# Swapping the two hardware DMA queues of a softmax kernel: loads on ScalarE, stores on Sync

## The chip, the cores and the metric

The kernel runs on one core of a Trainium2 chip. The metric is the device time of one execution in microseconds (us).

A ratio below is the mean time of one kernel's fast runs over the mean of the other kernel's fast runs in the same rounds on the same chip. It is therefore not quite the ratio of the medians quoted beside it. The range in brackets is its 95% interval.

## The reference

```python
# x: (16, 1024, 512) float32
x_scaled = x / 0.5
x_max = np.max(x_scaled, axis=-1, keepdims=True)
exp_x = np.exp(x_scaled - x_max)
return exp_x / np.sum(exp_x, axis=-1, keepdims=True)
```

This is a softmax over the last axis: 33.55 MB are read and as much is written.

## The kernel before

The 16384 rows are cut into eight chunks of 128 partitions x 16 rows x 512 elements (4096 KB each). Six buffers hold them, and everything is computed in place. Chunks 6 and 7 take the buffers of chunks 0 and 1, so their loads must wait until those have been stored. The last row of chunk 7 comes by a separate path on GpSimd.

```python
LOADS = [[(0, 4), (4, G)]] + [WHOLE] * 6 + [[(0, G - 1)]]
BLOCKS = [[(0, 4), (4, 8), (8, G)]] + [WHOLE] * 6 + [[(0, 8), (8, G)]]
STORES = [WHOLE] * 8
BUFS = 6
# ... (cut)
warm = stats.tile([P, 1], fp32, name="warm", bufs=1)
nc.vector.memset(warm, 0.0)
nc.scalar.activation(out=warm, in_=warm, func=EXP)      # table load happens here
# ... (cut)
def load(c):
    # ... (buffer chosen; cut)
    for lo, hi in LOADS[c]:
        part = nc.sync.dma_start(out=xt[:, lo:hi, :], in_=xr[c][:, lo:hi, :])

def shift(i):            # VectorE: -max of each row, times 2, is the bias
    if c not in chunks:
        load(c)
    nc.vector.tensor_reduce(negmax, rows_of_block, axis=AX, op=MAX, negate=True)
    nc.vector.tensor_scalar_mul(biases[i], negmax, 2.0)

def exponentials(i, rows):   # ScalarE: one row at a time, with its sum
    for g in rows:
        nc.scalar.activation(out=row, in_=row, func=EXP, bias=..., scale=2.0, accum_out=...)

def scale_vector(i):     # VectorE: 1/sum, and 14 of 16 rows times it
    k = b - b // 8
    nc.vector.reciprocal(...); nc.vector.tensor_mul(rows[:k], ...)

def scale_scalar(i):     # ScalarE: the other 2 of 16 rows ("copy rows")
    nc.scalar.activation(out=row, in_=row, func=COPY, scale=recip)

def store(i):
    nc.scalar.dma_start(out=outr[c][:, lo:hi, :], in_=chunks[c][:, lo:hi, :])

for i in range(n):
    exponentials(i + 1, rows(i + 1)[0])   # chunk 1: its first 14 rows
    scale_vector(i); scale_scalar(i)
    shift(i + 2)
    store(i)
    exponentials(i + 1, rows(i + 1)[1])   # chunk 1: its last 2 rows
```

(The bounds checks and slices of this excerpt are shortened.)

## Time and profile before

| | before |
|---|---|
| time, median of 6 runs (the first three had 161.77) | 161.81 us (161.71 to 162.05) |
| span of the profiled run | 160.5 us |
| VectorE (DVE) busy | 134.6 us |
| ScalarE (ACT) busy | 102.2 us |
| moved by DMA | 67.13 MB, 418 GB/s over the span |

How to read it: the share of a busy engine is no proof that it sets the time. These are lines of the view of waits in the kernel before; the columns are who waited and for whom, us in total, how often, and the longest:

```profile
ACT xt L108 <- DVE bias L81: 40.6, 10, 5.8
DVE negmax L77 <- DMA xt<-in_x_dram: 9.4, 2, 4.8
DVE recip L125 <- ACT xt L108: 1.8, 1, 1.8
```

ScalarE spends 40.6 us waiting for VectorE's biases (the idle time counted here includes its own DMA issues: the view does not count an issue as work). VectorE waits only for the first two loads and, at the very end, 1.8 us for ScalarE.

### The profile page before, as it was taken

The page shows a single profiled execution, that of the slowest core. Times are in us where ns is not written, and L with a number is a line of the kernel's source. Part 1 is how long each engine was busy: PE and PEld are TensorE (multiplying, and loading weights), DVE is VectorE, ACT ScalarE, POOL GpSimd, SP SyncE. Part 2 cuts the span into 40 slices and gives each one's busy share as a digit, 9 for nine tenths or more (in the row PEclk, how much of TensorE's full clock was granted, in tenths as well). Part 3 has the DMA queues.
Part 4 walks back from the last instruction along what each step waited for, and adds up shares of the span by engine and source line. Part 5 has one row for each costly group of instructions (what it writes and reads, how often), then busy time and mean ns, then how long its engine had stood idle before and what let it go on. Part 6 is the DMA issues. An engine that isn't in the chain of part 4 may idle for free.

```text
span 160.5 us, 411 instructions
## 1 busy us (share of the span) xinstructions
DVE 134.6 (84%) x45; ACT 102.2 (64%) x273; POOL 1.9 (1%) x7
## 2 busy tenths in 40 slices
DVE  0607999999999999999999999999999999957000
ACT  3071549069989963998199909991899891790000
POOL 0000000000000000000000000030000000000000
DMA  5999999999989999999999999989999999999994
GB/s 184 470 408 498 400 392 457 457 392 402 506 269 425 490 392 400 506 400 392 490 425 392 474 434 392 490 383 483 422 450 400 400 465 441 392 457 449 400 441 204
DMA packets 2578, 67.13 MB, mean 418 GB/s; under 512 B 328, under 2 KB 328, under 8 KB 400
## 3 DMA queue, kind: packets, MB, share of 16 engines
q1 hardware_dynamic: 1296, 33.29, 49.3%
q10 hardware_dynamic: 1152, 33.55, 48.4%
q0 software_dynamic: 128, 0.26, 0.4%
q14 instruction: 2, 0.02, 0.0%
HBM read 33.55 MB, written 33.55 MB: 418 GB/s over the span
## 4 chain that ended last, share of the span: by engine, by line
DVE 75%; DMA 7%; issue 5%; ACT 3%; SPq 0%
DVE negmax L77 42%; DVE xt L127 31%; DMA xt<-in_x_dram 7%; ACT xt L108 3%; DVE bias L81 1%; DVE recip L125 1%; SPq L68 0%
## 5 line engine op out<-in xcount | busy, mean ns | idle before, releaser
L108 ACT ACTIVATE xt<-xt,bias 128x512 f32<-128x512 f32 x128 | 90.4, 708 | 41.5 <-DVE bias L81 40.6
L77 DVE TENSOR_REDUCE negmax<-xt 128x16 f32<-128x8192 f32 (+2 forms) x11 | 69.9, 6352 | 9.4 <-DMA xt<-in_x_dram 9.4
L127 DVE TENSOR_TENSOR xt<-xt,recip 128x7168 f32<-128x7168 f32 (+2 forms) x11 | 62.0, 5637 | 0.4
L108 ACT ACTIVATION_READ_ACCUMULATOR xt<-xt,bias 128x1 f32 x128 | 23.9, 187 | 0.0
L138 ACT ACTIVATE xt<-xt,recip 128x512 f32<-128x512 f32 x15 | 9.9, 706 | 0.0
L125 DVE RECIPROCAL recip<-sums 128x16 f32<-128x16 f32 (+2 forms) x11 | 2.4, 218 | 1.8 <-ACT xt L108 1.8
L81 DVE TENSOR_SCALAR bias<-negmax 128x16 f32<-128x16 f32 (+2 forms) x11 | 1.9, 173 | 0.4
L52 ACT ACT_TABLE_LOAD x1 | 1.3, 1283 | 0.7 <-PEq L194 0.7
L97 POOL DMA_DIRECT2D xt<-in_x_dram x2 | 1.5, 741 | 0.5 <-issue 0.5
L90 POOL COPY seen<-sums 128x1 f32<-128x1 f32 x1 | 0.2, 184 | 103.6 <-ACT xt L108 103.6
L51 DVE MEMSET warm<- 128x1 f32 x1 | 0.1, 59 | 0.8 <-PEq L194 0.8
L52 ACT ACTIVATE warm<-warm 128x1 f32<-128x1 f32 x1 | 0.2, 202 | 0.0
L194 POOL MEMSET const-float32-0.0<- 128x1 f32 x1 | 0.1, 93 | 0.2 <-issue 0.2
L194 POOL MEMSET const-bfloat16-1.0<- 128x1 bf16 x1 | 0.1, 95 | 0.0
L194 POOL MEMSET const-uint8-127<- 128x1 uint8 x1 | 0.1, 95 | 0.0
L194 POOL MEMSET const-float32-1.0<- 128x1 f32 x1 | 0.1, 93 | 0.0
## 6 DMA issues: line engine op xcount, KB each, us to landing
out_dram<-xt ACTq DMA_DIRECT2D x8, 4096.0 KB, 23.1
xt<-in_x_dram SPq DMA_DIRECT2D x6, 4096.0 KB, 34.8
xt<-in_x_dram SPq DMA_DIRECT2D x1, 3840.0 KB, 27.8
xt<-in_x_dram SPq DMA_DIRECT2D x1, 3072.0 KB, 11.6
xt<-in_x_dram SPq DMA_DIRECT2D x1, 1024.0 KB, 4.8
xt<-in_x_dram POOLq DMA_DIRECT2D x1, 252.0 KB, 15.4
xt<-in_x_dram POOLq DMA_DIRECT2D x1, 4.0 KB, 9.1
```

The lines of the kernel that those rows point to most:

```text
L51: nc.vector.memset(warm, 0.0)
L52: nc.scalar.activation(out=warm, in_=warm, func=EXP)
L77: nc.vector.tensor_reduce(negmax[:, 0:b], chunks[c][:, lo:hi, :], axis=AX, op=MAX, negate=True)
L81: nc.vector.tensor_scalar_mul(biases[i][:, 0:b], negmax[:, 0:b], 2.0)
L90: copied = nc.gpsimd.tensor_copy(out=seen, in_=signal)
L97: part = nc.gpsimd.dma_start(out=to[p0:p1], in_=of_[p0:p1], max_dma_last_dim=2 * D)
L108: nc.scalar.activation(out=row, in_=row, func=EXP, bias=biases[i][:, g : g + 1], scale=2.0, accum_out=sums[i][:, g : g + 1],)
L125: nc.vector.reciprocal(recips[i][:, 0:b], sums[i][:, 0:b])
L127: last = nc.vector.tensor_mul(rows, rows, recips[i][:, 0:k].unsqueeze(2).broadcast_to((P, k, D)))
L138: last = nc.scalar.activation(out=row, in_=row, func=COPY, scale=recips[i][:, g : g + 1])
L194: nc = _bacc.Bacc("TRN2", target_bir_lowering=False, num_devices=1)
```

## The change

The intent is to let the two hardware queues change places. ScalarE issues all loads: the seven for chunks 0 to 5 as its first instructions, and the two that reuse buffers among its exponentials. Sync, which has nothing else to do, issues the stores, and can wait for them without holding up exponentials.

```diff
-    warm = stats.tile([P, 1], fp32, name="warm", bufs=1)
-    nc.vector.memset(warm, 0.0)
-    nc.scalar.activation(out=warm, in_=warm, func=EXP)
 ...
-            part = nc.sync.dma_start(out=xt[:, lo:hi, :], in_=xr[c][:, lo:hi, :])
+            part = nc.scalar.dma_start(out=xt[:, lo:hi, :], in_=xr[c][:, lo:hi, :])
 ...
+    RELOADS = {(3, 7): BUFS, (4, 11): BUFS + 1}
+    for c in range(BUFS):
+        load(c)
+    warm = stats.tile([P, 1], fp32, name="warm", bufs=1)
+    nc.vector.memset(warm, 0.0)
+    nc.scalar.activation(out=warm, in_=warm, func=EXP)
 ...
     def shift(i):
-        if c not in chunks:
-            load(c)
 ...
+            if (c, g) == (1, G - 3):
+                ahead.append(exponential.ins.name)
+            if (c, g) in RELOADS:
+                load(RELOADS[c, g])
 ...
-                part = nc.scalar.dma_start(
+                part = nc.sync.dma_start(
                     out=outr[c][:, lo:hi, :], in_=chunks[c][:, lo:hi, :]
                 )
+                if c == 0:
+                    tc.add_manual_dep(part.ins, ahead[0], info, reason="in step")
 ...
     for i in range(n):
         if i + 1 < n:
-            exponentials(i + 1, rows(i + 1)[0])
+            exponentials(i + 1, range(blocks[i + 1][2] - blocks[i + 1][1]))
 ...
-        if i + 1 < n:
-            exponentials(i + 1, rows(i + 1)[1])
```

## The prediction

> **What bounds the kernel now.** The kernel loads eight chunks of 4096 KB (4.194 MB), takes a softmax over each row, and stores them again: 33.55 MB in, 33.55 MB out. I first read the page of the profile for the busy shares and the DMA row. "VectorE is busiest, at 84%" would mislead on its own; the line of DMA tenths is 9 nearly everywhere, and the queue lines say that the two hardware queues are about equal, one of loads, one of stores.
>
> ```profile
> DVE 134.6 (84%) x45; ACT 102.2 (64%) x273; POOL 1.9 (1%) x7
> ...
> DMA  5999999999989999999999999989999999999994
> ...
> q1 hardware_dynamic: 1296, 33.29, 49.3%
> q10 hardware_dynamic: 1152, 33.55, 48.4%
> ```
>
> The reader is to see 49.3 + 48.4 + 0.4 = 98% of the time of 16 DMA engines filled with packets. Next I cut the span into stages (view of busy time by windows: the stretch, its length, the busy time of DVE, ACT and POOL, granted clock, DMA share, GB/s), to see whether DMA moves at one rate while it is busy.
>
> ```profile
> 0.00:4.00 4.00, 0.06 (x1) 1.49 (x2) 0.20 (x4) 1.00 0.57 184
> 4.00:44.00 40.00, 33.45 (x15) 22.13 (x61) 0.00 (x0) 1.00 1.02 438
> 44.00:52.00 8.00, 7.93 (x4) 7.28 (x22) 0.00 (x0) 1.00 0.92 340
> 52.00:112.00 60.00, 59.79 (x14) 44.75 (x121) 1.66 (x3) 1.00 1.00 433
> 120.00:156.00 36.00, 25.44 (x11) 19.35 (x50) 0.00 (x0) 1.00 1.01 436
> 156.00:160.50 4.50, 0.00 (x0) 0.00 (x0) 0.00 (x0) 1.00 0.52 226
> ```
>
> Loads alone (4 to 44 us), loads and stores together (52 to 112) and stores alone (120 to 156) all run at 433 to 438 GB/s. Only the start, the end, and the stage of the first store (44 to 52, 340 GB/s) lie below. 67.1 MB at 433 GB/s is 155.0 us; the span is 160.5 us. So about 5.5 us in all are ramp, end and dents, and the rest is the moving of bytes.
>
> Third, the chain that ended last, because a second bound might lie right beside the first one:
>
> ```profile
> by line: DVE negmax L77 41.8%; DVE xt L127 31.5%; DMA xt<-in_x_dram 7.2%; issue 5.4%; ACT xt L108 3.3%; DVE bias L81 1.1%; DVE recip L125 0.9%; SPq L68 0.2%
> ...
> 143.27 0.21 DVE recip L125
> 143.48 0.02 issue
> 143.50 3.89 DVE xt L127
> ```
>
> It runs through VectorE: from the second load's landing at 12.8 us VectorE works almost without a gap until 147.39 us, and the last store follows. That is a true chain too. The view of DMA issues, asked for the times of the last two stores, shows that both bounds meet there:
>
> ```profile
> out_dram<-xt ACTq DMA_DIRECT2D x1, 4096.0 KB, 17.0
> ...
> out_dram<-xt ACTq DMA_DIRECT2D x1, 4096.0 KB, 12.2
> ```
>
> The timeline puts their issues at 133.00 and 147.48 us, so they land at 150.0 and 159.7: 9.7 us apart, which is 4.194 MB at 433 GB/s. The last store was issued 2.5 us before the one ahead of it had landed, and its bytes follow with no gap. The queue therefore still sets the end, with VectorE within about 1 us of doing so (an estimate: the first load took 4.8 us from issue to landing for 1.05 MB, 2.4 us at 433 GB/s, so a transfer has up to 2.4 us of latency, part of it ramp; 2.5 us less 1.5 to 2.4).
>
> **What the Trainium skill says.** "DMA: Bandwidth & Descriptors", section "Issuing engines are not separate DMA queues": DMAs started by different engines "will ultimately run on the same 16 DMA engines and interleave with each other, regardless of the engine that started them"; a second issuer saves only sequencer time. The trace agrees as far as it can: an issue costs 0.33 to 0.67 us on Sync and 0.34 to 0.37 us on ScalarE, and loads alone from the one queue run as fast (438) as stores alone from the other (436). The same page, "Queues, rings and completion order", says each DMA engine takes turns between its queue rows, packet by packet. The trace agrees: with both queues filled a 4.194 MB transfer lands every 19.3 us (store 0 at 44.10 + 24.5 = 68.6, store 1 at 58.95 + 28.9 = 87.9), alone every 9.7. The same page, "Where 436 GB/s comes from", gives 435 GB/s as the ceiling of the core's ports; the 433 of the long stages is there already. "ScalarE: Activation LUTs", section "What ACT_TABLE_LOAD costs", gives about 1283 ns for a table load; the row of this trace says 1283 ns.
>
> **The change part by part.**
>
> 1. The seven loads of chunks 0 to 5 leave Sync for ScalarE, ahead of the warm-up. On Sync they begin at 0.74 us and take 3.53 us together by the timeline; ScalarE's first work begins at 0.74 us as well. First load: 0 us moved. The table load (1.28) and the warm-up exponential (0.20) then start near 4.3 and end near 5.8 us; the first true exponential waits for its bias until 8.05 us. Hidden with 2.2 us to spare: 0.
>
> 2. The eight stores leave ScalarE. Each cost it about 0.45 us (the timeline shows 0.45 us idle ahead of the row after store 0). It saves 8 x 0.45 = 3.6 us and pays 2 x 0.45 for the last two loads. ScalarE waits 40.6 us for the bias from VectorE, around 4.0 us ahead of each whole chunk, so time saved there only lengthens that wait: 0.
>
> 3. Store 0 moves later. Before, ScalarE does 14 rows of chunk 1, the copy row of chunk 0, issues the store (44.10), then does the other two rows. Now all 16 rows come first; two rows at 0.705 us pitch are 1.4 us, so store 0 goes at about 45.5 us. The new dependency on row 13 is met earlier than that and adds nothing. Loads 4 and 5 are still queued then (they land at 57.5 and 76.9), so the DMA engines have work either way: 0 on the end. Stores 0 and 1 land about 1.4 us later, near 70.0 and 89.3.
>
> 4. Load 6 waits for store 0, load 7 for store 1, and both waits now stop ScalarE. Before, Sync issued them at 68.67 and 88.02. Now load 6 comes after row 7 of chunk 3 (62.93 + 8 x 0.705 + 0.2 = 68.8 us) and load 7 after row 11 of chunk 4 (79.55 + 12 x 0.705 + 0.2 = 88.2). ScalarE stands for about 1.2 and 1.1 us, plus 0.45 each for the issue. The exponentials of chunk 3 ended at 74.2 and VectorE asks for the sums only at 79.4: 5 us of room, 1.7 used. Chunk 4 is the same. The store of the chunk before slips by those 1.7 us (75.6 to 77.3, 92.2 to 93.8), behind a store queue that is filled until 89 and 108. Load 6 still enters its queue behind load 5 (until about 76), load 7 behind load 6 (until about 96). No dry queue: 0.
>
> 5. The last stores are issued by Sync. The last one waits for VectorE's end at 147.39 on either engine; Sync answered a landed store with an issue 0.08 us later in this trace. 0 to +0.1 us.
>
> Sum: 161.77 + 0 to 0.1, which I put at 161.9 us.
>
> **The rivals.** (a) The compiler could put the table load ahead of the loads on ScalarE. The first load then starts 1.28 us late, and as DMA and VectorE both hang on it, the end goes to about 163.0. Against it: the table load's row belongs to the warm-up's line, and that line now stands after the loads. (b) ScalarE's stand for load 6 or 7 outgrows its room of 5 us, VectorE then waits for sums, and the tail moves beyond its 1 us: 163 to 165. It would need store 0 or 1 to land over 4 us later than computed; the fair sharing seen in the landings speaks against it. (c) The dent at the first store (340 GB/s for 8 us, (433 - 340) x 8 = 0.74 MB or 1.7 us by that view, which counts a packet at once and so exaggerates) may belong to the store queue's being ScalarE's, or to the moment: gone, the DMA path is about 1 us shorter and VectorE's chain then holds the end at about 160.8; doubled, 163. I expect it to come again, on the other queue. (d) The hoped-for gain: a freer ScalarE shortens the end. In the last block VectorE waits for it 1.8 us, but those exponentials wait for their own bias from 137.28 us, with no DMA issue among them: nothing.
>
> **Range and chances.** A gain over 2% needs 158.5 us or less. 67.1 MB at 433 GB/s plus the ramp at the start, with nothing else at all, is already about that, and the VectorE chain bars the way 1 us below today. A loss over 2% needs 165.0: rivals (a) and (c) together, or (b). Rivals (a) and (c) each alone stay within 1%. So: 161.9 us, 161.1 to 162.8 eight times in ten; faster 0.01, same 0.96, slower 0.03.
>
> **What would show it.** Right: the two long DMA stages again at about 433 GB/s with loads now on ScalarE's queue; first load issued at 0.74 and landed at 5.5 us; store 0 issued near 45.5; two new waits of ScalarE at its load issues of about 1 us each; VectorE's waits unchanged (9.4 us for loads, 1.8 us for sums) and its end near 147.4; last two landings 9.7 us apart. Wrong: a table load at 0.74 us ahead of the first issue; a wait of VectorE for exponentials in the middle; a stage where the DMA share falls below 0.9 other than at the first store; a last store that lands over 12.5 us after VectorE ended.

## The result, and the profile after

The changed kernel takes 161.82 us (median of 6 runs, 161.72 to 162.31) against 161.81 us (161.71 to 162.05). The ratio is 1.0004 [0.9988, 1.0019], so the time is the same.

The page of the changed kernel: VectorE's and ScalarE's busy time, the DMA tenths, and the two hardware queues (packets, MB, share of 16 engines' span).

```profile
DVE 134.6 (84%) x45; ACT 102.2 (64%) x273; POOL 1.9 (1%) x7
...
DMA  5999999999999999999999999899999999999993
...
q10 hardware_dynamic: 1296, 33.29, 49.0%
q1 hardware_dynamic: 1152, 33.55, 48.6%
```

The queues have traded names: the row with the loads (33.29 MB, 1296 packets) is now q10 and that with the stores q1. The share of the loads is 49.0% (49.3 before) and that of the stores 48.6% (48.4 before). The busy times are the same, and the DMA tenths differ in a few slices only.

The stages of the changed kernel, by the view of busy time in windows (stretch, length, busy DVE, ACT and POOL, granted clock, DMA share, GB/s):

```profile
4.00:44.00 40.00, 33.64 (x15) 23.81 (x65) 0.00 (x0) 1.00 1.02 439
44.00:52.00 8.00, 7.93 (x4) 7.16 (x20) 0.00 (x0) 1.00 1.01 393
52.00:112.00 60.00, 59.79 (x14) 44.78 (x120) 1.67 (x3) 1.00 1.00 433
120.00:156.00 36.00, 25.24 (x11) 19.04 (x50) 0.00 (x0) 1.00 1.01 435
```

The three long stages move at 439, 433 and 435 GB/s, against 438, 433 and 436 before. The stage of the first store is again below them. This view counts a packet in one place, so short windows scatter. Spreading each packet's bytes over its own duration gives 346 and 402 GB/s for the stretches 44 to 48 and 48 to 52 us before, and 412 and 363 after, against 433 around them: 0.47 MB and 0.36 MB not moved, worth 1.1 and 0.8 us.

The start, by the timeline of the changed kernel (start us, length us, engine, line, operation, tile):

```profile
0.74 3.48 ACTq L68 DMA_DIRECT2D xt<-in_x_dram  x7
...
4.25 1.28 ACT L80 ACT_TABLE_LOAD   x1 [4.25 <-issue]
...
7.87 0.72 ACT L117 ACTIVATE xt<-xt,bias 128x512 f32<-128x512 f32 x1 [2.11 <-DVE bias L90]
```

The loads go out at 0.74 us, as before, and the table load stands behind them. The first true exponential still waits 2.11 us for its bias, so the later table load cost nothing.

The waits of the changed kernel, in the columns explained above:

```profile
ACT xt L117 <- DVE bias L90: 35.7, 10, 5.5
DVE negmax L86 <- DMA xt<-in_x_dram: 9.2, 2, 4.8
...
ACT xt L117 <- DMA out_dram<-xt: 2.0, 2, 1.1
DVE recip L138 <- ACT xt L117: 1.8, 1, 1.8
```

A new wait of ScalarE has appeared: twice about 1 us, for a landed store and for the issue of the load behind it. What it waits for biases has fallen from 40.6 to 35.7 us. Most of that is at the start. This is the first exponential of the kernel before:

```profile
8.05 0.72 ACT L108 ACTIVATE xt<-xt,bias 128x512 f32<-128x512 f32 x1 [5.81 <-DVE bias L81]
```

Its wait of 5.81 us is now 2.11 us, because the issues of the loads and the table load fill the rest. The waits after the two new stands are 1.2 and 1.1 us shorter (4.01 us each before, 2.82 and 2.94 now), and two others are 0.6 us longer each. VectorE's two waits are the same within 0.2 us. ScalarE's work has been rearranged inside its own waiting time.

The last two stores of the changed kernel, by the view of DMA issues (the last column is us from issue to landing):

```profile
out_dram<-xt SPq DMA_DIRECT2D x1, 4096.0 KB, 16.8
...
out_dram<-xt SPq DMA_DIRECT2D x1, 4096.0 KB, 12.0
```

They are issued at 132.79 and 147.26 us, so they land at 149.6 and 159.2 us: 9.7 us apart as before, one transfer right behind the other.

### The profile page after: what moved, and what is told of

Read it like the earlier page. It is cut to its first block, busy times and chain, and to the rows that moved or that the text cites. A ratio compares the mean times of both kernels' runs of the same rounds, so it can differ in the third digit from the quotient of the medians.

```text
span 160.1 us, 413 instructions
## 1 busy us (share of the span) xinstructions
DVE 134.6 (84%) x45; ACT 102.2 (64%) x273; POOL 1.9 (1%) x7
## 3 DMA queue, kind: packets, MB, share of 16 engines
q10 hardware_dynamic: 1296, 33.29, 49.0%
q1 hardware_dynamic: 1152, 33.55, 48.6%
## 4 chain that ended last, share of the span: by engine, by line
DVE 75%; DMA 7%; issue 5%; ACT 3%; ACTq 0%
DVE negmax L86 42%; DVE xt L140 32%; DMA xt<-in_x_dram 7%; ACT xt L117 3%; DVE bias L90 1%; DVE recip L138 1%; ACTq L68 0%
## 5 line engine op out<-in xcount | busy, mean ns | idle before, releaser
L117 ACT ACTIVATE xt<-xt,bias 128x512 f32<-128x512 f32 x128 | 90.4, 707 | 37.8 <-DVE bias L90 35.7
L80 ACT ACT_TABLE_LOAD x1 | 1.3, 1283 | 4.3 <-issue 4.3
```

What stands on the lines that cost most here:

```text
L117: exponential = nc.scalar.activation(out=row, in_=row, func=EXP, bias=biases[i][:, g : g + 1], scale=2.0, accum_out=sums[i][:, g : g + 1],)
```

## The experiments

The theory to test: the stream of bytes sets the end, from the first load's issue on. VectorE follows it closely, and ScalarE has about 5 us of room per chunk. Each part of the change fits into this room, so each part is free by itself. The rivals: VectorE's chain sets the end, as the chain view draws it; parts of the change cost and gain, and cancel; the wait of ScalarE for a store is hidden only by luck; the dent at the first store belongs to the queue.

All edits are made to the changed kernel. All results were correct.

### e8: the swap alone undone

```diff
-            part = nc.scalar.dma_start(out=xt[:, lo:hi, :], ...)
+            part = nc.sync.dma_start(out=xt[:, lo:hi, :], ...)
-                part = nc.sync.dma_start(out=outr...)
+                part = nc.scalar.dma_start(out=outr...)
```

> The changed kernel with the two queues swapped back (loads on Sync, stores on ScalarE), all else of the change kept, so store 0 stays behind 16 rows of chunk 1. Theory (each part of the change is free by itself): 161.8 (161.4 to 162.2), ScalarE without the two waits of about 1 us for landed stores, its 40 us of waits for VectorE back. Rival (the swap costs or gains something that the other parts cancel): off 161.8 by more than 0.5 us.

Measured: 161.97 us (161.75 to 162.24) against 161.82, ratio 1.0008 [0.9996, 1.0020]. The waits of ScalarE in this run:

```profile
ACT xt L117 <- DVE bias L90: 41.1, 10, 5.8
```

Its wait for landed stores is gone and the 5 us are back in its wait for biases (3.7 of them at the first exponential, which waits 5.80 us again). The swap costs and gains nothing beyond 0.2%. What remains of the change (store 0 behind all 16 rows of chunk 1) was not run beside the kernel before; the two ratios together put it at nothing within about 0.3%. No cost and gain were cancelling to more than that.

### e9: the added dependency removed

```diff
-                if c == 0:
-                    tc.add_manual_dep(part.ins, ahead[0], info, reason="in step")
```

> The changed kernel without the added dependency of store 0 on row 13 of chunk 1. Theory (the copy row of chunk 0, which stands behind all 16 rows on ScalarE, already holds store 0 back, so the dependency adds nothing): store 0 issued at the same 45.3 to 45.8 us, time 161.8 (161.4 to 162.2). Rival (it holds store 0 back): store 0 issued over 1 us earlier.

Measured: 161.71 us (161.69 to 161.94) against 161.85, ratio 0.9995 [0.9981, 1.0008]. The timeline of this run, after row 15 of chunk 1 and the copy row of chunk 0:

```profile
44.79 0.71 ACT L151 ACTIVATE xt<-xt,recip 128x512 f32<-128x512 f32 x1
45.52 0.38 SPq L161 DMA_DIRECT2D out_dram<-xt  x1
```

Store 0 goes out right behind the copy row, as with the dependency (there the copy row began at 44.57 and the store at 45.30). The dependency adds nothing.

### e2: VectorE relieved of two more rows per chunk

```diff
-        k = b - b // 8
+        k = b - b // 4
-        for g in range(b - b // 8, b):
+        for g in range(b - b // 4, b):
```

> The changed kernel with 4 of 16 rows scaled on ScalarE in place of 2: VectorE loses two rows of 0.545 us a whole chunk. Theory (the stream of bytes sets the end): VectorE ends its last multiply several us before 147.1, at about 138 to 142, and the time stays at 161.8 (161.3 to 162.1). Rival (VectorE's chain sets the end, as the chain view draws it): the time falls with VectorE, to about 155 to 157 us.

Measured: 162.12 us (162.01 to 162.70) against 161.89, ratio 1.0016 [0.9999, 1.0032]. The last piece of the chain that ended last (start us, us, what), and the last two stores, in this run:

```profile
137.09 3.36 DVE xt L140
```

```profile
out_dram<-xt SPq DMA_DIRECT2D x1, 4096.0 KB, 19.6
...
out_dram<-xt SPq DMA_DIRECT2D x1, 4096.0 KB, 18.9
```

VectorE ends at 140.45 us in place of 147.19, 6.7 us earlier. The last store is issued 6.7 us earlier too and takes 18.9 us in place of 12.0 to land. Its landing, at 159.4 us, is where it was. The chain view draws its line through VectorE in both kernels; this run shows that in the changed kernel it is not what sets the time. The time, 162.12 us, is at the upper edge of what the theory expected, and far from the 155 to 157 us of the rival.

### e4 and e5: VectorE delayed ahead of its last multiply

```diff
+        if i == n - 1:
+            extra = stats.tile([P, 4], fp32, name="extra", bufs=1)     # e5: 1 in place of 4
+            nc.vector.tensor_reduce(extra, chunks[c][:, lo : lo + 4, :], axis=AX, op=MAX, negate=True)
```

> The changed kernel with one more reduction over 4 rows (2.29 us) on VectorE right before its last multiply; its result is not used. Theory (DMA sets the end with about 0.3 to 1.2 us of room ahead of VectorE's end): last store issued 2.3 us later, and only 1.1 to 2.0 us of it shows: 162.9 to 163.8 us. Rival 1 (VectorE's chain sets the end now): all of it shows, 164.1. Rival 2 (there is 2.5 us of room, the time between the last issue and the landing of the store before): 161.8.

> As the run with 4 rows more on VectorE ahead of its last multiply (which cost 2.2 us of VectorE and 1.6 us of time, so about 0.5 us of room), here with 1 row, about 0.55 us. Theory (DMA sets the end with about half a microsecond of room): last store issued 0.55 us later, time 161.8 to 162.1. Rival (VectorE's end counts in full): 162.4.

Measured: e4 163.53 us (163.51 to 163.66) against 161.89, ratio 1.0098 [1.0082, 1.0114]; e5 162.16 us (162.03 to 162.73) against 161.82, ratio 1.0025 [1.0013, 1.0036]. The chain of e4 around the addition, and its last store:

```profile
143.39 2.16 DVE extra L142
145.57 3.89 DVE xt L145
```

```profile
out_dram<-xt SPq DMA_DIRECT2D x1, 4096.0 KB, 11.1
```

Of 2.16 us added to VectorE, 161.89 x 0.0098 = 1.6 us show in the time. But the time holds more than the span of the core. Time less span is 1.72 to 1.84 us in every listed run of the changed kernel, of e1, e2, e3, e8, e9 and e11, and 2.01 to 2.14 us in every run of e4, e5, e6 and e7 (e10 has both). Why is not known. By the mean span, e4 costs 161.50 - 160.18 = 1.3 us, so about 0.85 of the 2.16 us did not show.

The queue says the same. The last store of e4, issued when its queue is empty, lands in 11.1 us; in the changed kernel it took 12.0, so there it waited 0.9 us for the store ahead of it. That is the room. By the same measure it is 0.4 to 1.1 us in the profiles of the kernel before, e1, e6, e8 and e9, which change nothing at the end.

In e5 VectorE ended at 148.06 us, 0.87 later than in the profile of the changed kernel: 0.56 for the added row, and most of the rest because the first load landed 0.28 us later in that execution. Yet the last store landed at 159.24 us in both, after 11.1 us in e5: VectorE has just caught up with the stream. The mean span is 0.1 us longer. The time is 0.2 to 0.6 us longer, between the two expectations, and by itself would not tell them apart; most of that lies outside the span. Beside e2 the picture is plain: earlier by 6.7 us gains nothing, later by 2.2 us costs 1.3 us of span.

### e11 and e3: ScalarE made to stand longer

```diff
-    RELOADS = {(3, 7): BUFS, (4, 11): BUFS + 1}
+    RELOADS = {(3, 0): BUFS, (4, 0): BUFS + 1}       # e11
+    RELOADS = {(2, 8): BUFS, (4, 11): BUFS + 1}      # e3
```

> The changed kernel with the last two loads behind row 0 of chunks 3 and 4 in place of rows 7 and 11, so ScalarE stands for store 0 from about 63.5 to 69.1 and for store 1 from about 82.6 to 88.4. Theory (about 5 us of room): VectorE waits about 1.0 us for the sums of chunk 3 and 2.8 us for those of chunk 4, ends 3.8 us later; less the 0.5 us of room at the end, the time is 164.4 to 165.5 us. Rival (a stand under 6 us a chunk is free): 161.8.

> The changed kernel with load 6 issued after row 8 of chunk 2 in place of row 7 of chunk 3, so ScalarE stands from about 52.6 us until store 0 has landed at about 69.1. Theory (ScalarE's room before VectorE asks for its sums is about 5 us; beyond it the stand goes one for one into VectorE's chain and then to the end): VectorE waits about 12 us for exponentials of chunk 2, ends near 159 instead of 147.1, time 172 to 175 us. Rival (a wait beside a full DMA queue is always hidden): time 161.8.

Measured: e11 165.03 us (164.71 to 165.40) against 161.85, ratio 1.0195 [1.0179, 1.0212]; e3 173.3 us, a single run of unknown state, against 161.89. From the timeline of e11, the two moments at which VectorE asks for the sums of chunks 3 and 4; the last brackets hold its idle time just before and what ended it:

```profile
80.53 0.25 DVE L138 RECIPROCAL recip<-sums 128x16 f32<-128x16 f32 x1 [1.04 <-ACT xt L117]
...
99.83 0.25 DVE L138 RECIPROCAL recip<-sums 128x16 f32<-128x16 f32 x1 [2.59 <-ACT xt L117]
```

and from that of e3, the same for chunk 2:

```profile
74.94 0.25 DVE L138 RECIPROCAL recip<-sums 128x16 f32<-128x16 f32 x1 [11.90 <-ACT xt L117]
```

VectorE's new waits are 1.04 and 2.59 us where 1.0 and 2.8 were expected, and 11.90 where 12 was. So the room of ScalarE is what the timeline said, about 5 us a chunk: the stand less the wait that it caused is 6.10 - 1.04 = 5.1 us for chunk 3 of e11 and 16.95 - 11.90 = 5.05 us in e3. (For chunk 4 of e11 it is 6.70 - 2.59 = 4.1 us, because its exponentials began late, behind the stand of chunk 3.) Beyond the room, a stand goes one for one into VectorE's chain, and from there, less the room at the end, into the time: in e11 VectorE ends at 151.19 us in place of 147.19, 4.0 us later, 3.6 of them in these two waits. The last store lands at 162.35 us in place of 159.24, 3.1 us later, which is 4.0 less 0.9. The time is 161.85 x 0.0195 = 3.2 us longer. The swap is free because rows 7 and 11 were chosen well, and not because a wait beside a full queue is free as such.

### e1: the warm-up put back ahead of the loads

```diff
+    warm = stats.tile([P, 1], fp32, name="warm", bufs=1)
+    nc.vector.memset(warm, 0.0)
+    nc.scalar.activation(out=warm, in_=warm, func=EXP)
     for c in range(BUFS):
         load(c)
-    warm = stats.tile([P, 1], fp32, name="warm", bufs=1)
-    nc.vector.memset(warm, 0.0)
-    nc.scalar.activation(out=warm, in_=warm, func=EXP)
```

> The changed kernel with the warm-up (table load 1.28 us, first exponential 0.20 us) put back ahead of the loads on ScalarE. Theory (the start of the first load moves both the DMA stream and VectorE's chain, and ScalarE's loads wait for what stands before them): first issue at about 2.2 us in place of 0.74, first load landed near 6.8 in place of 5.3, time about 163.2 us (162.9 to 163.5). Rival 1 (ScalarE's sequencer issues a DMA past a running table load): first issue still below 1.2 us, time 161.8. Rival 2 (the start has slack): first issue late, yet the time within 0.3 us of 161.8.

Measured: 162.43 us (161.94 to 162.72) against 161.89, ratio 1.0029 [1.0010, 1.0047]. The start of its timeline:

```profile
0.74 1.28 ACT L76 ACT_TABLE_LOAD   x1 [0.74 <-PEq L198]
...
0.91 1.34 ACTq L68 DMA_DIRECT2D xt<-in_x_dram  x3
2.03 0.20 ACT L76 ACTIVATE warm<-warm 128x1 f32<-128x1 f32 x1
```

The expectation of the theory fell and the first rival's mechanism held. The table load runs from 0.74 to 2.02 us, and ScalarE's sequencer issues three loads beside it, the first at 0.91: only 0.17 us late. "Perfetto Trace Analysis", section "Sequencer Loop", in the Trainium skill says that the sequencer pushes an engine instruction into a queue and reads on; this trace agrees for the table load, and the expectation had neglected it. The time is still 0.2 to 0.8 us longer by its interval. A start 0.17 us late explains a part of it at most; the first load landed at 5.60 us, inside the 5.32 to 5.64 us of the runs with the loads first. Whether the rest is more than scatter is open.

### e6 and e7: the store queue used once at the start

```diff
+    prime = stats.tile([P, D], fp32, name="prime", bufs=1)
+    nc.vector.memset(prime[0:16, :], 0.0)
+    primed = nc.sync.dma_start(out=outr[0][0:16, 0, :], in_=prime[0:16, :])
 ...
+                    tc.add_manual_dep(part.ins, primed.ins.name, info, reason="same rows")   # store 0
```

e7 adds the edit of e2.

> The changed kernel with a first store of 32 KB (zeros, which store 0 overwrites later) on Sync at about 1 us, before any load has landed. It tests what makes the dent in the rate at the first store (44 to 52 us, about 393 GB/s by the windows in the changed kernel, about 0.35 MB or 0.8 us lost). Theory A (first use of the store queue makes it): the dent moves to the start, the stage runs at 430 or more, the DMA stream is up to 0.8 us shorter, of which about 0.5 us can show because VectorE then sets the end: 161.3. Theory B (stores coming in among loads make it, used before or not): the dent stays, time 161.8.

> The primed kernel with 4 of 16 rows scaled on ScalarE as well, so that VectorE cannot set the end. If theory A of the priming holds, the whole 0.8 us shows: 161.0 to 161.3. If theory B holds: 162.1, as the run with fewer rows on VectorE alone.

Measured: e6 162.19 us (162.01 to 162.80) against 161.82, ratio 1.0032 [1.0019, 1.0046]; e7 162.21 us (162.11 to 162.54), ratio 1.0026 [1.0014, 1.0038]. Neither shows the gain of theory A; e7 is where theory B put it, e6 0.4 us above. The stage of the first store in e6, by windows:

```profile
44.00:52.00 8.00, 7.93 (x4) 7.16 (x20) 0.00 (x0) 1.00 1.02 397
```

397 against 393 GB/s without priming; by packets, 423 and 360 GB/s in the two halves, 0.33 MB not moved. The dent is still there, so the first use of a queue does not make it. In e8, with the stores on ScalarE's queue, it measures 405 and 343 GB/s, 0.47 MB as in the kernel before: it comes on either queue, when stores begin among loads. The packets of the changed kernel show more: the DMA engines do not stand idle in the dent (packets fill 100% of their time in both halves). About 30 load packets of 32 KB, started between 47.0 and 49.1 us, take 1.4 to 1.9 us each, where the usual one takes 1.21; the packets of the store take 1.21 as everywhere. Why these load packets take longer stays open. The priming itself costs 0.3%, but two thirds of that lie outside the core's span (mean span 160.22 against 160.08 us, mean time 162.30 against 161.85), as in e4, e5 and e7; the cause was not tested.

### e10: chunk 7 loaded whole, without GpSimd

```diff
-    LOADS = [[(0, 4), (4, G)]] + [WHOLE] * 6 + [[(0, G - 1)]]
+    LOADS = [[(0, 4), (4, G)]] + [WHOLE] * 6 + [WHOLE]
-            if c == BUFS - 1 and g == 10:
-                load_last_row(sums[i][:, g : g + 1])
```

with the edit of e2, so that VectorE could not hide a gain.

> The changed kernel with 4 of 16 rows scaled on ScalarE (which alone measured 162.1) and with chunk 7 loaded whole by ScalarE's queue, without GpSimd's separate last row. Theory (the bytes set the end, and GpSimd's small packets take DMA time for about 0.27 MB of other bytes at 112 to 120 us): stage 112 to 120 runs at 430 or more, the last landing comes about 0.6 us sooner, 161.3 to 161.7. Rival (that dent is the change from reading to writing and stays): 162.1.

Measured: 162.24 us (161.82 to 162.38) against 161.85, ratio 1.0018 [1.0005, 1.0032]. The gain did not come, because the loss that it was to win back was never there. By packets of the two hardware queues, the halves of the stretch from 112 to 120 us run at 389 and 409 GB/s in the changed kernel and at 433 in e10, and 0.27 MB seem to be missing. But this leaves out GpSimd's own queue. It is this line on the page of the changed kernel, and e10 has none:

```profile
q0 software_dynamic: 128, 0.26, 0.4%
```

These 0.26 MB, the last row, are moved almost wholly in this stretch, at 43 and 22 GB/s. All queues together run at 432 and 431 GB/s, against 433 in e10. So GpSimd's small packets keep at most 0.01 MB of other bytes from moving, worth 0.03 us, and in e10 the same bytes come by ScalarE's queue. The expectation was missed because its premise was wrong. Its rival named about the right time, 162.1 us, but it too took the dent for real. The last store lands at 159.47 us, and in e2, which differs from e10 by this edit alone, at 159.44.

## Why the prediction was right

It said 161.9 us, 161.1 to 162.8, and the same with a chance of 0.96. Measured was 161.82.

- **The bound.** That the stream of bytes sets the end, with VectorE about 1 us behind, is shown from both sides: e2 (VectorE 6.7 us earlier, nothing gained) and e4 (2.2 us later, 1.3 us of span lost). The room is 0.9 us in the profile of the changed kernel, 0.4 to 1.1 in the others.
- **Step 1, the loads first on ScalarE.** Issued at 0.74 us, table load and warm-up from 4.25 to 5.75 us, first exponential waiting for its bias: as worked out.
- **Step 2, the stores off ScalarE.** No change of the total, as e8 shows for the swap. But the step said that the time saved would lengthen ScalarE's wait for biases, and that wait fell, from 40.6 to 35.7 us: an issue counts as idle time in this view already before, so dropping the stores shows only in two waits (0.27 to 0.84 and 4.62 to 5.22 us), and the loads' issues and the two stands take more away than that.
- **Step 3, store 0 later.** Issued at 45.30 us (about 45.5 expected), landed at 69.1 (near 70.0), so it landed 0.5 us later than before and not 1.4. Why is not settled; in this profile the first load landed 0.18 us earlier and the dent was shallower (0.36 MB in place of 0.47). The statement that the new dependency adds nothing is shown by e9.
- **Step 4, ScalarE stands for the last two loads.** Two waits of 1.07 and 0.96 us. They include the issue of the load, so they stand against the 1.2 + 0.45 and 1.1 + 0.45 us of the step's sum: too much by 0.6 us each, because stores 0 and 1 landed 0.9 us earlier than worked out (69.09 and 88.42 us against 70.0 and 89.3). The stores behind them went out at 76.55 and 93.05 us, where 77.3 and 93.8 were worked out. It did not matter. The room of 5 us is shown by e11 and e3.
- **Step 5, the last store on Sync.** Issued 0.07 us after VectorE's end; nothing lost.
- **Rival (a)** was mis-sized: with the table load first, the loads start 0.17 us late and not 1.28 us, because they are issued beside it (e1).
- **Rival (c)** was left open between a dent that belongs to the queue and one that belongs to the moment. It came again on the other queue, as expected, and priming the queue does not remove it.

No version tried is faster than either kernel beyond the noise: the lowest, e9, is 0.9995 [0.9981, 1.0008] of the changed kernel.

## What to carry to other kernels

Where the DMA engines move at one rate from the first load to the last store, as in this kernel at 433 GB/s, expect that who issues a transfer matters only if it changes when the engines have work. Look for a stage in which the queue would run dry, not for the engine that is busiest. An engine that waits a lot can take over a wait, but only up to the room until its consumer asks: read that room off the timeline before placing a blocking issue in its stream, and test the placement by moving it a few rows. To tell two bounds that meet at the end apart, move one of them both ways: relieve it, and delay it. Before a loss in a DMA stage is blamed on a queue, count the bytes of every queue, that of GpSimd too. For effects of a few tenths of a microsecond, look at the spans beside the times.

## What the Trainium skill lacked or had wrong

- "DMA: Bandwidth & Descriptors" does not describe the loss when stores begin among loads: with all engines busy, the rate fell from 433 GB/s to between 343 and 423 in the two 4 us stretches around the first store (0.3 to 0.5 MB lost), on either queue, primed or not.
- The same page, section "Where 436 GB/s comes from", says that the HBM side, about 358 GB/s, binds for transfers between HBM and SBUF. Here one core moved 433 GB/s for 60 us, loads and stores mixed. Read alone, the sentence is wrong for such a kernel; the page's own remark just above it, that its 425 GB/s was measured with the pair's other core idle and that two streaming cores get about half the domain each, fits.
- "ScalarE: Activation LUTs", section "What ACT_TABLE_LOAD costs", adds a drain of about 1380 ns to the 1283 ns of a load for a switch of sets. This kernel loads only one table, the first, so no run shows a switch; behind this one no drain is seen: the warm-up exponential starts at 5.55 us, 0.02 us after the load's end (4.25 + 1.28).
- No page looked at says outright that DMA issues pass a running table load on the same engine; here the first came 0.17 us into the 1.28 us (e1). It follows from the general description of the sequencer.
